# Gate modulation sums moved into the attention steps, and a negated causal mask applied together with the row extreme, in a two-layer trunk on one Trainium2 core

## The chip, the cores and the metric

The kernel runs on one core of a Trainium2 chip. That core has a matrix engine (PE, whose weight loads the profile lists as PEld), a vector engine (DVE), a scalar engine (ACT), a general engine (POOL) and a sync engine (SP), which here issues most of the DMAs; sixteen DMA engines carry the transfers. The metric is the device time of one execution in microseconds (us), lower being better, as the median of three runs.

## The reference

Two layers over a sequence of 512 tokens of width 2048, batch 1, all in f32. Layer 1 is a multi-scale retention, layer 2 a latent attention; each is one residual sub-layer, and shift, scale and gate of each layer come from a conditioning vector c of 2048 numbers.

```
mod  = silu(c) @ ada_w[i] + ada_b[i]          # shift, scale, gate of layer i
h    = rmsnorm(x, g) * (1 + scale) + shift
x    = x + gate * branch(h)                   # branch: retention, or attention
```

The attention (16 heads, 128 "nope" and 64 rotary dimensions a head, values of 128) is

```
q  = rmsnorm(cq) @ w_uq ; k_nope, v = split(rmsnorm(ckv) @ w_ukv)
s  = (q @ k.T) * 192 ** -0.5
s  = where(key_pos <= query_pos, s, -1e30)
o  = softmax(s) @ v
out = (silu(g) * o) @ w_out
```

The gate of layer 2 is a vector of 2048 numbers, each a sum of 2048 products of silu(c) with a column of ada_w.

## The kernel before

The program is written step by step, and the issue order on every engine is the order in which the steps are written; `queued(...)` writes one operation down, and `behind(engine)` puts an operation where that engine's queue stands. f32 products are made from a high and a low part, so nearly every matmul comes three times (`mm3`, lines L158 to L160) and a tile that feeds PE is first split by ACT (high part, L1937) and DVE (low part, L1938: the source less the high part).

Layer 2's attention works on pairs of heads. `attention_step(pr)` treats heads 2pr and 2pr+1 and, between their parts, makes the projections of the next pair, nx = pr + 1. `attention_step(-1)`, in which there are no heads yet, makes only the projections of pair 0; then follow steps 0 to 6. The last pair's heads are interleaved with the output projection, which ends the kernel.

The projections of a pair are seven PSUM tiles, in this order: uq_2 (the rotary part of both heads' q), uq_0, uq_1 (the other q), uk_0, uk_1 (k) and uv_0, uv_1 (v). They take turns on four PSUM buffers ("acc"), so uk_1 takes the buffer of uq_2, uv_0 that of uq_0 and so on. The rotation of uq_2 is three pieces: `rope_own` (DVE, L1949: qr_t = uq_2 * cos), `rope_swap` (ACT, L1944: four copies of 32 rows from uq_2 into qr_sw) and `rope_turn` (DVE, L1953 and L1954: qr_sw * sin, then the sum). The buffer of uq_2 is free when both qr_t and the four copies have read it. In the built program the first of the four copies waits for qr_t.

A head's scores s fill four PSUM tiles a_0 to a_3 (query blocks of 128 rows, 128 to 512 key columns; "aux" buffers). For each, DVE adds the 128x128 causal mask to the block on the diagonal (L2084) and takes the negated row maximum (L2086), and ACT makes exp(s + that) with the row sums (L2087). After the four tiles come the reciprocals (L2091), the normalisation, the transposes on PE, their split (pt, L1937 and L1938) and the products with v.

Layer 2's gate is made from ada_w's transpose: 16 blocks of 128 outputs by two halves of 1024 inputs are 32 tiles of 128x1024 (512 KB, `mod_gate`, two buffers), each loaded by SP (L2153) and multiplied by the half of silu(c) that stands in `c_gate` (broadcast to 128 rows, loaded by L2147) and summed along the row by one DVE operation (`gate_sum`, L2157). The first 16 sums ("part 0") stand in the attention steps -1 to 6, two in each, ahead of the two splits of the values (`part_values`) at the step's end; their loads are issued at the step's start. The other 16 ("part 1") stand in the output projection (`o2_hooks`).

Of the kernel before, what the change touches and what calls it, by code (L numbers as in the profile page):

```python
# [49 lines left out]
def hybrid_trunk_kernel(  # L50
# [25 lines left out]
    nc = tc.nc  # L76
    PE, ACT, DVE, POOL = nc.tensor, nc.scalar, nc.vector, nc.gpsimd
# [17 lines left out]
    def big(name, dt=F32R):  # L95
        return base.tile([P, 2, T], dt, tag="big", bufs=16, name=name)
# [19 lines left out]
    ident = base.tile([P, P], F32, name="ident")  # L116
    make_identity(nc, ident)
    mask = base.tile([P, P], F32, name="mask")
    make_causal_mask(nc, mask, mask_val=-1e30)
    ones = base.tile([P, P], F32, name="ones")  # L120
    DVE.memset(ones, 1.0)
    few = base.tile([P, 2 * NT], F32, name="few")
# [92 lines left out]
    qn_c, kvn_c = vcol[:, 128:132], vcol[:, 132:136]  # L215
# [244 lines left out]
    A_, V_, T_, S_ = (getattr(mybir.EngineType, e) for e in ("Activation", "DVE", "PE", "SP"))  # L460

    @contextmanager
    def behind(*engines):

        with ExitStack() as stack:
            for e in engines:
                ins = next((i for i in reversed(nc.cur_bb.bb.instructions) if i.engine == e), None)
                if ins is not None:
                    stack.enter_context(tc.issue_after(ins))
            yield  # L470

    def queued(fn, *args):
        with behind(A_, V_, T_, S_):
            return fn(*args)
# [256 lines left out]
    for u in range(1, NU):  # L731

        here, there = ("v", "qk") if u % 2 == 0 else ("qk", "v")
# [989 lines left out]
    def l2_tile(tag, bufs, name, shape=(P, T), dt=F32):  # L1723
        return pools["l2"].tile(list(shape), dt, tag=tag, bufs=bufs, name=name)
# [121 lines left out]

    def latent_norm(n):
        if n == "q":
            DVE.tensor_scalar(out=qn_s, in0=qn_c, scalar1=192.0**-0.5, scalar2=None, op0=ALU.mult)
        ss = small(f"ss_{n}", NT)  # L1850
        for t in range(NT):
            ACT.activation(tmp(f"{n}_sq{t}"), latent[n][t], AF.Square, accum_out=ss[:, t : t + 1])
        latent[n, "ss"] = ss
# [207 lines left out]
    def attend(h):  # L2061

        pr, s = h // 2, h % 2
        own = heads2[pr]
        ps, p_, nb, pt, side = [], [], [], [], {}

        def scores(i):
            n = (i + 1) * P
            ps.append(aux(f"a_{h}_{i}"))
            qn, kn, qr = own["uq", s, "T"], own["uk", s, "T"], own["qr"]  # L2070
            mm3(ps[i][:, :n], act_block(qn, i), (kn[:, 0, :n], kn[:, 1, :n]), True, False)
            for a in range(2):
                PE.matmul(ps[i][:, :n], qr[:, s, i * P : n], krope[0][:, a, :n], start=False, stop=a == 1)

        def exps(i):
            n = (i + 1) * P
            if i == 0:
                side["sm"] = small(f"sm_{h}", NT)
                if s == 0:
                    p_.extend(l2_tile("pp", 5, f"p_{h}_{j}") for j in range(NT))  # L2080
                else:
                    both = l2_pair(f"p_{h}_").bitcast(F32)
                    p_.extend(both[:, j * T : (j + 1) * T] for j in range(NT))
            DVE.tensor_add(ps[i][:, i * P : n], ps[i][:, i * P : n], mask)  # L2084
            nb.append(small(f"nb_{h}_{i}"))
            DVE.tensor_reduce(out=nb[i], in_=ps[i][:, :n], axis=AX.X, op=ALU.max, negate=True)  # L2086
            ACT.activation(p_[i][:, :n], ps[i][:, :n], AF.Exp, bias=nb[i], accum_out=side["sm"][:, i : i + 1])  # L2087

        def reciprocals():
            side["rs"] = small(f"rs_{h}", NT)  # L2090
            DVE.reciprocal(side["rs"], side["sm"])  # L2091

        def normalise():
            for i in range(NT):
                v, r = p_[i][:, : (i + 1) * P], side["rs"][:, i : i + 1]
                if s == 0:
                    ACT.activation(v, v, AF.Identity, scale=r)
                else:
                    DVE.tensor_scalar(out=v, in0=v, scalar1=r, scalar2=None, op0=ALU.mult)

        place = [(0, 0), (1, 0), (2, 0), (1, 384)]

        def transposes():
# [25 lines left out]

        def result():  # L2130
            o2 = l2_tile("o2", 2, f"o2_{h}")
            DVE.tensor_mul(o2, side["o"], side["sg"])
            POOL.dma_start(o2_d[h * P : (h + 1) * P, :], o2)

        return scores, exps, lambda: (queued(reciprocals), queued(normalise)), transposes, split_pt, load_gate, values, result

    gate_c_half = {}
    gate_sums = [base.tile([P, 2, 8], F32, tag="mod_c", bufs=2, name=f"gate_sums{i}") for i in range(2)]  # L2140

    def gate_load(part, n):

        j, b = n // 8, n % 8
        if b == 0:
            half = gate_c_half[j] = big(f"c_gate{part}{j}", F32)
            nc.sync.dma_start(  # L2147
                half.rearrange("p a n -> p (a n)"),
                c_d[0:1, j * 1024 : (j + 1) * 1024].rearrange("o n -> (o n)").partition_broadcast(P),
            )  # L2150
        aw = l2_tile("bw", 2, f"mod_gate_{part}{b}{j}", (P, 2, T))
        r0 = 2 * D + (8 * part + b) * P
        nc.sync.dma_start(aw, ada_t[1, r0 : r0 + P, j * 1024 : (j + 1) * 1024].rearrange("p (a n) -> p a n", a=2))  # L2153
        return aw, part, j, b, gate_c_half[j]

    def gate_sum(aw, part, j, b, c_half):
        DVE.scalar_tensor_tensor(  # L2157
            out=aw, in0=aw, scalar=1.0, in1=c_half, op0=ALU.mult, op1=ALU.mult,
            accum_out=gate_sums[part][:, j, b : b + 1],
        )  # L2160
        if (j, b) == (1, 7):
            use_modulation(1, 2, part, gate_sums[part])

    def attention_step(pr):

        nx = pr + 1
        here = [attend(2 * pr + s) for s in range(2)] if pr >= 0 else ()
        both = heads2[nx] = {}
        units_ahead()
        with behind(S_):  # L2170
            sums = [gate_load(0, 2 * nx + i) for i in range(2)]
        if here:
            (sc0, ex0, no0, tr0, sp0, lg0, va0, re0), (sc1, ex1, no1, tr1, sp1, lg1, va1, re1) = here
            queued(lg0)
# [7 lines left out]
        low()  # L2182
        if here:
            no0()
        queued(uq_products, nx, 2)
        if here:
            for i in range(NT):
                queued(sc1, i)
            for i in range(NT):
                queued(ex1, i)  # L2190
        t1 = queued(rope_own, both["uq", 2], f"qr_{nx}")
        low = next_unit("ukv") if here else lambda: None
        if here:
            no1()
        low()
        for b in range(2):
            queued(uq_products, nx, b)
        sw = queued(rope_swap, both["uq", 2], f"qr_{nx}")
# [26 lines left out]
            queued(uv_products, nx, j, (1,))  # L2225
        for j in range(2):
            queued(uv_products, nx, j, (0, 2, 3))
            queued(gate_sum, *sums[j])
            queued(queued(part_values, nx, j))
        if here:  # L2230
            queued(va1)
# [3 lines left out]
        krope.append(big("kr"))  # L2235
        split(kr["f"], krope[0][:, 0, :], krope[0][:, 1, :])

    first = Step(multiply=lambda: (queued(krope_parts), attention_step(-1)))
    first.units = [unit("ukv", 0, 0)]
    steps[-1].units += [unit("uq", 0, u) for u in range(2)]  # L2240
    steps.append(first)
# [121 lines left out]
    o2_in, o2_res = {}, {}  # L2363
    N_ENDS = 5

    gate_pending, gate_n = [], [0, 0]

    def o2_hooks(i):
        l2_hooks.get(i, lambda: None)()
        with behind(V_):  # L2370
            while gate_pending:
                gate_sum(*gate_pending.pop())
        with behind(S_):
            for _ in range(min(1, 16 - gate_n[0]) if 4 < i and i > gate_n[1] else 0):
                gate_pending.insert(0, gate_load(1, gate_n[0]))
                gate_n[0] += 1
        gate_n[1] = i

    def o2_parts(r, u):
        if u not in o2_in:  # L2380
# [235 lines left out]
```

## Time and the profile before

| what | value |
|---|---|
| three runs | 2119.31, 2120.16, 2120.32 us; median 2120.16 us |
| profiled execution, span of the core | 2118.4 us |
| PE busy | 2104.0 us (99%) |
| DVE busy | 1676.0 us (79%) |
| ACT busy | 1055.5 us (50%) |
| attention_step(-1) on PE | about 1677 to 1696.5 us |
| steps 0 to 6 | about 1697.5 to 1918.6 us |
| output projection with the last pair | about 1918.6 to 2106 us |

The page gives no time of its own for the profiled execution beside its span; the span is 1.8 us under the median of the runs, which is time around the span. In the answers of the trace, a timeline row is: start, duration, engine, line, operation, tile written from tiles read, shapes, count, and, in brackets, for how long the engine sat idle before it and what ended that. A DMA's row on SP is its issue and not its transfer; how long the transfer took from its issue until it had landed is a row of another view. Matmuls overlap in the records, so PE's steps are read from their starts.

### The profile page before, as it was taken

Reading aid. Unit: us, or ns where it says so; the run is one execution under the profiler, and the core shown is the slowest. Engines: PE = TensorE matmul, PEld = TensorE weight load, DVE = VectorE, ACT = ScalarE, POOL = GpSimd, SP = SyncE. Lnnn points to the kernel's source line nnn. Section 1 sums busy time; section 2 is a strip of 40 time slices with the busy share of each in tenths; the row PEclk is TensorE's granted clock in tenths of the full one; section 3 lists DMA queues with packets and bytes.
Section 4 is the critical chain, followed back from the end, with each engine's and each line's share of the span. In section 5 each row is a group of like instructions: output and inputs, shape, how many; then the busy total and the mean of one; then the engine's idle time right before and its main releaser. Section 6 shows DMA issues by size and latency. Waiting matters only on the chain.

```text
span 2118.4 us, 30062 instructions
## 1 busy us (share of the span) xinstructions
PE 2104.0 (99%) x11124; PEld 1812.6 (86%) x11124; DVE 1676.0 (79%) x2506; ACT 1055.5 (50%) x1622; POOL 103.6 (5%) x176
## 2 busy tenths in 40 slices
PE   8999999999999999999999999999999999999998
PEld 6888898989889888888888888898889989888888
DVE  7899888888888789666777778768978788886665
ACT  6765444444454444434344444345446575664443
POOL 1001010000000000000000000010001000000000
PEclk9999999999999999999999999999999999999999
DMA  9975786868787778856657556753566644346643
GB/s 381 406 280 195 248 276 222 283 211 272 239 263 250 242 229 283 265 172 196 222 173 241 201 198 230 258 191 108 164 189 209 190 129 149 118 137 219 222 142 138
DMA packets 230101, 462.95 MB, mean 219 GB/s; under 512 B 20881, under 2 KB 84401, under 8 KB 226369
## 3 DMA queue, kind: packets, MB, share of 16 engines
q1 hardware_dynamic: 217312, 421.07, 60.3%
q0 software_dynamic: 11920, 38.91, 4.7%
q8 instruction: 87, 1.43, 0.3%
q10 hardware_dynamic: 722, 1.06, 0.2%
q14 instruction: 60, 0.49, 0.1%
HBM read 417.96 MB, written 43.00 MB: 218 GB/s over the span
## 4 chain that ended last, share of the span: by engine, by line
PE 96%; DMA 1%; DVE 1%; ACT 0%; issue 0%; SPq 0%; DVEq 0%
PE o L1486 16%; PE o L2450 4%; PE x L884 2%; PE x L883 2%; PE x L885 2%; PE y L885 2%; PE y L884 2%; PE s L885 2%; PE s L884 2%; PE s L883 2%; PE y L883 2%; PE uv L2046 2%; PE qk L158 2%; PE s_qk L984 2%; PE x_qk L984 2%; PE qk L160 2%
## 5 line engine op out<-in xcount | busy, mean ns | idle before, releaser
L1486 PE MATMUL o<-o_h,o_p 128*128 128x512 f32 (+1 forms) x1088 | 323.0, 378 | 0.0
L1486 PEld LDWEIGHTS o<-o_h,o_p 128*128 128x128 f32 x1088 | 200.2, 188 | 37.1
L1486 PE MATMUL o<-o_l,o_p 128*128 128x512 f32 (+1 forms) x544 | 204.8, 376 | 0.0
L136 DVE TENSOR_TENSOR o_p<-o_r,o_p 128x1024 fp32r<-128x1024 f32 x64 | 78.1, 1222 | 54.3 <-ACT o_p L135 54.1
L1486 PEld LDWEIGHTS o<-o_l,o_p 128*128 128x128 f32 x544 | 102.3, 188 | 18.3
L2450 PE MATMUL o<-o_h,o_w 128*128 128x512 f32 (+1 forms) x336 | 82.7, 337 | 0.0
L1170 DVE SCALAR_TENSOR_TENSOR mod<-mod,c_odd 128x1024 f32<-128x1024 f32 x56 | 67.2, 1219 | 15.3 <-DMA mod<-in_ada_t_dram 15.3
L135 ACT CAST o_p<-o_r 128x1024 fp32r<-128x1024 f32 x64 | 66.7, 1054 | 22.4 <-PE o L1486 13.3
L158 PE MATMUL qk<-hT,qk_p 128*128 128x512 f32 x192 | 75.0, 391 | 0.0
L160 PE MATMUL qk<-hT,qk_p 128*128 128x512 f32 x192 | 74.9, 390 | 0.0
L389 DVE SCALAR_TENSOR_TENSOR aw<-aw,c_all 128x2048 f32<-128x2048 f32 (+1 forms) x37 | 73.2, 1997 | 2.1 <-DMA aw<-in_ada_t_dram 2.1
L159 PE MATMUL qk<-hT,qk_p 128*128 128x512 f32 x192 | 74.7, 389 | 0.0
L2450 PEld LDWEIGHTS o<-o_h,o_w 128*128 128x128 f32 x336 | 57.7, 188 | 6.9
L2450 PE MATMUL o<-o_l,o_w 128*128 128x512 f32 (+1 forms) x168 | 56.5, 337 | 0.0
L136 DVE TENSOR_TENSOR o_l<-o_in,o_h 128x1024 fp32r<-128x1024 f32 x24 | 29.3, 1222 | 34.2 <-ACT o_h L135 34.2
L1332 ACT ACTIVATE yn<-y,nmr,gn_r 128x512 f32<-128x512 f32 x32 | 22.3, 778 | 67.7 <-DVE nmr L1326 67.7
L135 ACT CAST o_h<-o_in 128x1024 fp32r<-128x1024 f32 x24 | 25.3, 1052 | 61.6 <-PE o L159 40.5
L158 PE MATMUL o<-o_h,o_w 128*128 128x512 f32 x128 | 50.1, 391 | 0.0
L160 PE MATMUL o<-o_h,o_w 128*128 128x512 f32 x128 | 49.8, 389 | 0.0
L159 PE MATMUL o<-o_l,o_w 128*128 128x512 f32 x128 | 49.8, 389 | 0.0
L1170 DVE SCALAR_TENSOR_TENSOR mod<-mod,c_bm 128x1024 f32<-128x1024 f32 x40 | 48.7, 1219 | 0.0
L448 PE MATMUL g<-hT,g_p 128*128 128x512 f32 x192 | 46.1, 389 | 0.0
(1532 smaller groups left out, 6238.3 us busy)
## 6 DMA issues: line engine op xcount, KB each, us to landing
mod<-in_ada_t_dram SPq DMA_DIRECT2D x96, 512.0 KB, 5.7
o_r<-in_ret_w_out_dram SPq DMA_DIRECT2D x64, 512.0 KB, 5.5
aw<-in_ada_t_dram SPq DMA_DIRECT2D x28, 1024.0 KB, 9.5
mod_gate<-in_ada_t_dram SPq DMA_DIRECT2D x32, 512.0 KB, 4.4
o_w_raw<-in_mla_w_out_dram SPq DMA_DIRECT2D x32, 512.0 KB, 4.4
qk_r<-in_ret_w_in_dram SPq DMA_DIRECT2D x48, 256.0 KB, 3.5
qk_r<-qk_d SPq DMA_DIRECT2D x32, 256.0 KB, 6.1
v_r<-v_d SPq DMA_DIRECT2D x32, 256.0 KB, 5.7
```

The costliest lines, as they stand in the source:

```text
L135: ACT.copy(hi, src)
L136: DVE.tensor_sub(lo, src, hi.bitcast(F32))
L158: PE.matmul(o, lhs[0], rhs[0], start=first and not seeded, stop=False, skip_group_check=seeded)
L159: PE.matmul(o, lhs[0], rhs[1], start=False, stop=False, skip_group_check=seeded)
L160: return PE.matmul(o, lhs[1], rhs[0], start=False, stop=last, skip_group_check=seeded)
L883: PE.matmul(banks[b], a[0], w[0], start=first, stop=False, skip_group_check=True)
L884: PE.matmul(banks[b], a[0], w[1], start=False, stop=False, skip_group_check=True)
L885: PE.matmul(banks[b], a[1], w[0], start=False, stop=True, skip_group_check=True)
L984: PE.matmul(o, w[wp][:, i, b * P : (b + 1) * P], a[ap], start=first and i + b + k == 0, stop=k == 2, skip_group_check=True,)
L1170: DVE.scalar_tensor_tensor(out=aw, in0=aw, scalar=1.0, in1=silu_c[j], op0=ALU.mult, op1=ALU.mult, accum_out=row_sums[piece][:, j, b : b + 1],)
L1486: PE.matmul(o, w[i][:, ki, c0 + b * P : c0 + (b + 1) * P], a[j], start=first and i + j == 0, stop=last and i == 1, skip_group_check=True,)
L2450: PE.matmul(banks2[b][:, cols], w[0][i][:, 0, b * P : (b + 1) * P], o2_moving(w, u, cols)[j], start=u + i + j == 0, stop=u == KD - 1 and i ...
```

## The change

Three things are changed in layer 2.

First, q is scaled by the negated factor, so that the score tiles hold negated scores; the mask holds +1e30, and one DVE operation (`tensor_tensor_reduce`) adds a mask to all columns of the tile, in place, and takes the row minimum, in place of L2084 and L2086; the exponential takes scale -1. The mask for all widths is one tile `masks` of 384 columns of zeros and 128 columns of the causal mask, of which each query block reads the last n columns. It stands in one of the five buffers "pp", which hold p of a pair's first head, and is filled in step -1 by a POOL memset and an ACT copy. In the order of the program the new operation is a row `ISA` with the tile, and a second with the row extreme (`nb`) alone.

Second, all 32 gate sums are in steps -1 to 6, four in each: the first ahead of the products of uq_2, the second in the middle of the second head's four mask operations, and the third and fourth where the two stood before. In step -1, where there are no heads, the first two follow each other.

Third, the loads follow a list: up to two tiles are on their way at a time, issued at the step's start, in its middle and behind each of the third and fourth sums. The 32 tiles go through one half of c for both parts and then through the other, so c_gate is loaded twice and not four times.

```diff
@@ def latent_norm(n)
-            DVE.tensor_scalar(out=qn_s, in0=qn_c, scalar1=192.0**-0.5, scalar2=None, op0=ALU.mult)
+            DVE.tensor_scalar(out=qn_s, in0=qn_c, scalar1=-(192.0**-0.5), scalar2=None, op0=ALU.mult)
@@ def attend(h), exps(i)
-            DVE.tensor_add(ps[i][:, i * P : n], ps[i][:, i * P : n], mask)
             nb.append(small(f"nb_{h}_{i}"))
-            DVE.tensor_reduce(out=nb[i], in_=ps[i][:, :n], axis=AX.X, op=ALU.max, negate=True)
-            ACT.activation(p_[i][:, :n], ps[i][:, :n], AF.Exp, bias=nb[i], accum_out=side["sm"][:, i : i + 1])
+            DVE.tensor_tensor_reduce(
+                out=ps[i][:, :n], in0=ps[i][:, :n], in1=masks[0][:, T - n :], scale=1.0, scalar=3e38, op0=ALU.add,
+                op1=ALU.min, accum_out=nb[i],
+            )
+            ACT.activation(
+                p_[i][:, :n], ps[i][:, :n], AF.Exp, bias=nb[i], scale=-1.0, accum_out=side["sm"][:, i : i + 1]
+            )
@@ gate loads and sums
-    def gate_load(part, n):
-        j, b = n // 8, n % 8
-        if b == 0:
-            half = gate_c_half[j] = big(f"c_gate{part}{j}", F32)
+    gate_n, gate_pending = [0], []
+    def gate_load():
+        n = gate_n[0]
+        j, part, b = n // 16, n // 8 % 2, n % 8
+        if n % 16 == 0:
+            half = gate_c_half[j] = big(f"c_gate{j}", F32)
...
+    def gate_loads():
+        with behind(S_):
+            while gate_n[0] < 32 and len(gate_pending) < 2 and not (gate_n[0] % 16 == 0 and gate_pending):
+                gate_load()
+
+    def gate_sum():
+        aw, part, j, b, c_half = gate_pending.pop(0)
         DVE.scalar_tensor_tensor(
...
+    def make_masks():
+        masks.append(l2_tile("pp", 5, "masks"))
+        POOL.memset(masks[0][:, : T - P], 0.0)
+        ACT.copy(masks[0][:, T - P :], mask)
@@ def attention_step(pr)
-        with behind(S_):
-            sums = [gate_load(0, 2 * nx + i) for i in range(2)]
+        gate_loads()
...
         if here:
             no0()
+        queued(gate_sum)
         queued(uq_products, nx, 2)
         if here:
             for i in range(NT):
                 queued(sc1, i)
-            for i in range(NT):
+            for i in range(2):
+                queued(ex1, i)
+        queued(gate_sum)
+        if here:
+            for i in range(2, NT):
                 queued(ex1, i)
         t1 = queued(rope_own, both["uq", 2], f"qr_{nx}")
         low = next_unit("ukv") if here else lambda: None
         if here:
             no1()
         low()
+        gate_loads()
...
         for j in range(2):
             queued(uv_products, nx, j, (0, 2, 3))
-            queued(gate_sum, *sums[j])
+            queued(gate_sum)
+            gate_loads()
             queued(queued(part_values, nx, j))
@@ def o2_hooks(i)
-        with behind(V_):
-            while gate_pending:
-                gate_sum(*gate_pending.pop())
-        with behind(S_):
-            for _ in range(min(1, 16 - gate_n[0]) if 4 < i and i > gate_n[1] else 0):
-                gate_pending.insert(0, gate_load(1, gate_n[0]))
-                gate_n[0] += 1
-        gate_n[1] = i
```

The first place is DVE's queue in step -1, from the split of the rotary key (kr) to the split of uq_0. Before:

```order
L136 TENSOR_TENSOR kr<-kr_f,kr 128x512
L1938 TENSOR_TENSOR ukv_1_p<-ukv_1_r,ukv_1_p 128x2x256 x2
L1949 TENSOR_TENSOR qr_t_15096<-uq_2_15083,cos_12566 128x512
L1953 TENSOR_TENSOR qr_sw<-qr_sw,sin_12568 128x512
L1954 TENSOR_TENSOR qr_t_15096<-qr_t_15096,qr_sw 128x512
L1938 TENSOR_TENSOR uqT_0_15129<-uq_0_15098,uqT_0_15129 128x512
```

The same place with the change:

```order
L136 TENSOR_TENSOR kr<-kr_f,kr 128x512
L1938 TENSOR_TENSOR ukv_1_p<-ukv_1_r,ukv_1_p 128x2x256 x2
L2170 SCALAR_TENSOR_TENSOR mod_gate_15075,gate_sums_1426<-mod_gate_15075,c_gate_15073 128x1024
L2170 SCALAR_TENSOR_TENSOR mod_gate_15077,gate_sums_1426<-mod_gate_15077,c_gate_15073 128x1024
L1949 TENSOR_TENSOR qr_t_15101<-uq_2_15087,cos_12566 128x512
L1953 TENSOR_TENSOR qr_sw<-qr_sw,sin_12568 128x512
L1954 TENSOR_TENSOR qr_t_15101<-qr_t_15101,qr_sw 128x512
L1938 TENSOR_TENSOR uqT_0_15138<-uq_0_15107,uqT_0_15138 128x512
```

Two gate sums now stand between the split of ukv_1 and qr_t, and so ahead of everything that follows on DVE in this step. SP's queue from this step's start is, with the change (c_gate, here `L2153`, stands third in both kernels, behind the step's first two mod_gate tiles; the two mod_gate tiles behind ukv_0 are the third and fourth of the step):

```order
L2159 DMA mod_gate_15075<-in_ada_t_dram 128x1024
L2159 DMA mod_gate_15077<-in_ada_t_dram 128x1024
L2153 DMA c_gate_15073<-c_d 128x1024
L1974 DMA ukv_0_r<-in_mla_w_ukv_dram 128x2x512
L2159 DMA mod_gate_15103<-in_ada_t_dram 128x1024
L2159 DMA mod_gate_15105<-in_ada_t_dram 128x1024
L1974 DMA ukv_1_r<-in_mla_w_ukv_dram 128x2x512
L1974 DMA uq_0_r<-in_mla_w_uq_dram 128x2x384
```

The second pair of mod_gate tiles stood behind uq_0 before, and now stands between two loads of projection weights.

The second place is DVE's queue in a pair's step (step 1), from the reciprocals of the first head to the rotation of the next pair. Before:

```order
L2091 RECIPROCAL rs_15670<-sm_15645 128x4
L2084 TENSOR_TENSOR a_0_15689<-a_0_15689,mask 128x128
L2086 TENSOR_REDUCE nb_0_15716<-a_0_15689 128x1
L2084 TENSOR_TENSOR a_1_15695<-a_1_15695,mask 128x128
L2086 TENSOR_REDUCE nb_1_15720<-a_1_15695 128x1
L2084 TENSOR_TENSOR a_2_15701<-a_2_15701,mask 128x128
L2086 TENSOR_REDUCE nb_2_15724<-a_2_15701 128x1
L2084 TENSOR_TENSOR a_3_15707<-a_3_15707,mask 128x128
L2086 TENSOR_REDUCE nb_3_15728<-a_3_15707 128x1
L1949 TENSOR_TENSOR qr_t_15731<-uq_2_15676,cos_12566 128x512
```

With the change, where `ISA` is the new mask operation and `L2170` the gate sum:

```order
L2095 RECIPROCAL rs_15673<-sm_15652 128x4
L2170 SCALAR_TENSOR_TENSOR mod_gate_15576,gate_sums_1427<-mod_gate_15576,c_gate_15073 128x1024
L2085 ISA a_0_15693,nb_0_15719<-a_0_15693,masks 128x128
L2085 ISA nb_0_15719 128x1
L2085 ISA a_1_15699,nb_1_15722<-a_1_15699,masks 128x256
L2085 ISA nb_1_15722 128x1
L2170 SCALAR_TENSOR_TENSOR mod_gate_15600,gate_sums_1427<-mod_gate_15600,c_gate_15073 128x1024
L2085 ISA a_2_15705,nb_2_15726<-a_2_15705,masks 128x384
L2085 ISA nb_2_15726 128x1
L2085 ISA a_3_15711,nb_3_15729<-a_3_15711,masks 128x512
L2085 ISA nb_3_15729 128x1
L1949 TENSOR_TENSOR qr_t_15732<-uq_2_15680,cos_12566 128x512
```

Two operations a score tile have become one with its read-out, and two sums have come in ahead of qr_t.

More of the change, by code (lines that the diff above doesn't have):

```diff
@@ L118, in hybrid_trunk_kernel @@
     mask = base.tile([P, P], F32, name="mask")
-    make_causal_mask(nc, mask, mask_val=-1e30)
+    make_causal_mask(nc, mask, mask_val=1e30)
     ones = base.tile([P, P], F32, name="ones")
@@ L2153, in gate_load @@
         nc.sync.dma_start(aw, ada_t[1, r0 : r0 + P, j * 1024 : (j + 1) * 1024].rearrange("p (a n) -> p a n", a=2))
-        return aw, part, j, b, gate_c_half[j]
-    def gate_sum(aw, part, j, b, c_half):
+        gate_n[0] += 1
+        gate_pending.append((aw, part, j, b, gate_c_half[j]))
+    def gate_loads():
[4 more added lines that the diff above has]
+        aw, part, j, b, c_half = gate_pending.pop(0)
         DVE.scalar_tensor_tensor(
@@ L2162, in gate_sum @@
             use_modulation(1, 2, part, gate_sums[part])
+    masks = []
+    def make_masks():
+        masks.append(l2_tile("pp", 5, "masks"))
+        POOL.memset(masks[0][:, : T - P], 0.0)
+        ACT.copy(masks[0][:, T - P :], mask)
     def attention_step(pr):
@@ L2236, in krope_parts @@
         split(kr["f"], krope[0][:, 0, :], krope[0][:, 1, :])
-    first = Step(multiply=lambda: (queued(krope_parts), attention_step(-1)))
+    first = Step(multiply=lambda: (queued(krope_parts), queued(make_masks), attention_step(-1)))
     first.units = [unit("ukv", 0, 0)]
@@ L2364, in hybrid_trunk_kernel @@
     N_ENDS = 5
-    gate_pending, gate_n = [], [0, 0]
     def o2_hooks(i):
         l2_hooks.get(i, lambda: None)()
-        with behind(V_):
-            while gate_pending:
-                gate_sum(*gate_pending.pop())
-        with behind(S_):
-            for _ in range(min(1, 16 - gate_n[0]) if 4 < i and i > gate_n[1] else 0):
-                gate_pending.insert(0, gate_load(1, gate_n[0]))
-                gate_n[0] += 1
-        gate_n[1] = i
     def o2_parts(r, u):
```

## The prediction

> **What bounds the kernel now.** I read the page's busy shares first, then two stretches of the trace (a pair's step; the output projection), then all of PE's waits.
>
> ```profile
> PE 2104.0 (99%) x11124; PEld 1812.6 (86%) x11124; DVE 1676.0 (79%) x2506; ACT 1055.5 (50%) x1622; POOL 103.6 (5%) x176
> ...
> 1760.69:1792.27 31.58, 31.58 (x195) 28.43 (x194) 26.07 (x54) 20.02 (x46) 1.08 (x2) 1.00 0.45 142
> 1918.56:2060.00 141.44, 141.44 (x651) 118.26 (x650) 94.52 (x126) 63.57 (x87) 1.63 (x3) 1.00 0.59 196
> ...
> PE c_ps L474 <- DMA c_all<-in_c_dram: 3.2, 1, 3.2
> PE xT_ps L474 <- DVE x_diag L571: 2.2, 3, 1.2
> PE v L448 <- DVE hT L423: 0.9, 1, 0.9
> PE y L158 <- DVE o_l L1366: 0.3, 1, 0.3
> PE x_sums L2483 <- ACT x_sq L2422: 0.2, 1, 0.2
> ```
>
> The second and third rows are stretches: length, then busy time of PE, PEld, DVE, ACT and POOL, granted clock, DMA share. A pair's step is 31.58 us long and PE is busy through all of it at clock 1.00; DVE is busy for 26.07. The output projection is PE from end to end too. The last five rows are all of PE's waits in the whole run, 6.8 us together, and only the 0.2 at the very end lies behind the touched code. So PE sets the end everywhere that the change reaches: DVE work taken away is worth nothing there, and only a new PE wait can move the time.
>
> **The change part by part.** First place, step -1. DVE's, ACT's, SP's and PE's rows of it before:
>
> ```profile
> 1680.62 1.29 DVE L1938 TENSOR_TENSOR ukv_p<-ukv_r,ukv_p 128x512 fp32r<-128x512 f32 x2
> 1681.82 0.68 DVE L1949 TENSOR_TENSOR qr_t<-uq,cos 128x512 f32<-128x512 f32 x1
> ...
> 1686.26 1.28 DVE L1938 TENSOR_TENSOR uqT<-uq,uqT 128x512 fp32r<-128x512 f32 x2
> ...
> 1682.54 2.35 ACT L1944 COPY qr_sw<-uq 32x512 f32<-32x512 f32 x4 [1.52 <-DVE qr_t L1949]
> ...
> 1687.99 0.39 PE L160 MATMUL uk<-kvT,ukv_p 128*128 128x512 f32 x1
> 1688.22 0.39 PE L158 MATMUL uk<-kvT,ukv_p 128*128 128x512 f32 x1
> ...
> 1676.05 2.12 SPq L2153 DMA_DIRECT2D mod_gate<-in_ada_t_dram  x2
> 1678.21 0.49 SPq L2147 DMA_DIRECT2D c_gate<-c_d  x1
> 1681.93 0.38 SPq L1974 DMA_DIRECT2D ukv_r<-in_mla_w_ukv_dram  x1
> ```
>
> PE's row at 1688.22 is the first of uk_1, which takes uq_2's buffer; the one ahead is the last of uk_0. The buffer is free when ACT's four copies into qr_sw are done, and ACT's row says what these waited for: 1.52 us, for qr_t. Before, qr_t started at 1681.82 and the copies ended at 1682.54 + 2.35 = 1684.89, 3.3 us ahead of uk_1. The change puts two gate sums ahead of qr_t, and the first needs mod_gate and c_gate. When have those landed? Transfers around c_gate's issue, each with its time from issue to landing, and last the landings known for c_gate in the whole run (three of its four):
>
> ```profile
> mod_gate<-in_ada_t_dram SPq DMA_DIRECT2D x1, 512.0 KB, 7.1
> ...
> mod_gate<-in_ada_t_dram SPq DMA_DIRECT2D x1, 512.0 KB, 7.8
> ...
> ukv_r<-in_mla_w_ukv_dram SPq DMA_DIRECT2D x1, 512.0 KB, 7.4
> ...
> DMA to landing us min/median/max: 5.6/5.6/8.0
> ```
>
> The two mod_gate tiles, issued at 1676.05 and just before 1678.2 (I take 1677.7), landed at 1683.15 and about 1685.5; ukv_r, the transfer behind c_gate, issued at 1681.93, landed at 1689.33. They landed in order of issue, so c_gate lies between 1685.5 and 1689.3. The two mod_gates are 2.35 apart; one such step behind the second is 1687.85, my value. The sums' own time comes from two that follow each other at once:
>
> ```profile
> 33.24 1.22 DVE L389 SCALAR_TENSOR_TENSOR aw<-aw,c_all 128x1024 f32<-128x1024 f32 x1
> 34.38 0.08 DVE L389 DVE_READ_ACCUMULATOR aw<-aw,c_all 128x1 f32 x1
> 34.38 1.22 DVE L389 SCALAR_TENSOR_TENSOR aw<-aw,c_all 128x1024 f32<-128x1024 f32 x1
> ```
>
> 1.14 us from start to start, so 2.3 for two. Then: sums from 1687.85, qr_t at 1690.2 instead of 1681.82, the first copy 0.72 later as before (1682.54 - 1681.82) at 1690.9, all four done at 1693.25, uk_1 at 1693.3 instead of 1688.22. **PE stands for 5.1 us**; with the landing at its bounds, 2.75 to 6.55. Late next: DVE's splits of uq_0 and uq_1, which free the buffers of uv_0 and uv_1. They come 8.4 us later, the first done at about 1686.26 + 0.64 + 8.4 = 1695.3, and uv_0 starts behind uk_1's 12 matmuls of 0.227 us, at 1696.0: 0.7 to spare. Behind that PE has no idle time that could give 5.1 us back, so it reaches the end.
>
> Second place, steps 0 to 6. Groups over those seven steps and the page's row of a wide product:
>
> ```profile
> L2086 DVE TENSOR_REDUCE nb<-a 128x1 f32<-128x128 f32 (+3 forms) x56 | 27.5, 491 | 1.9
> ...
> L2157 DVE SCALAR_TENSOR_TENSOR mod_gate<-mod_gate,c_gate 128x1024 f32<-128x1024 f32 x14 | 17.0, 1214 | 0.0
> L2084 DVE TENSOR_TENSOR a<-a,mask 128x128 f32<-128x128 f32 x56 | 16.7, 297 | 10.5 <-PE a L2073 9.0
> ...
> L136 DVE TENSOR_TENSOR o_p<-o_r,o_p 128x1024 fp32r<-128x1024 f32 x64 | 78.1, 1222 | 54.3 <-ACT o_p L135 54.1
> ```
>
> Removed a step: 8 x 0.297 + 8 x 0.491 = 6.30 us. Added: two sums, 2.28, and eight of the new operation, which no row shows. From below it is a reduction of the same columns and a read-out, 0.491 + 0.08: 4.57 for eight. From above, twice that pass, as if the sum and the minimum took the columns one after the other: 0.98 + 0.08, 8.5 for eight. I take the lower end, since a one-pass sum with a row sum (1.214 for 1024 columns) costs no more than a plain product (1.222). DVE goes from 26.07 to 26.6 us of 31.58, or to 30.55 at the upper end: hidden by PE either way, with 5.0 or 1.0 to spare.
>
> [...]
>
> Within a step, what is late is qr_t, and with it all that DVE does up to pt, the transposed probabilities:
>
> ```profile
> 1765.16 0.17 DVE L2091 RECIPROCAL rs<-sm 128x4 f32<-128x4 f32 x1
> ...
> 1776.72 1.61 DVE L1938 TENSOR_TENSOR pt<-pT,pt 128x512 fp32r<-128x512 f32 x3
> ...
> 1780.76 0.39 PE L158 MATMUL o<-pt,v 128*128 128x512 f32 x1
> ...
> 1755.11 3.56 SPq L2153 DMA_DIRECT2D mod_gate<-in_ada_t_dram  x2
> ...
> DMA to landing us min/median/max: 4.1/4.6/5.8
> ...
> 1773.51 8.31 SPq L1974 DMA_DIRECT2D ukv_r<-in_mla_w_ukv_dram  x2
> ```
>
> pt is done at 1778.33, 2.4 us ahead of the first product that reads it. Up to there the mask operations of both heads save 6.30 - 4.57 = 1.7 and the two sums cost 2.3: 0.6 late, inside 2.4. The first two sums (behind the reciprocal, 1765.3) read tiles issued at 1755.11 and 3.3 us later; landings of mod_gate in these steps take 4.1 to 5.8 (the last row but one), so they are there by 1764.2. The next two tiles are issued in the step's middle, where the buffers come free by 1768, behind ukv_r's first issue at 1773.51, and land by 1780; their sums stand at 1785. SP queues one load of weights behind them, two issues or 0.7 us later.
>
> The negated scale, the exponential's scale and the mask's fill in step -1 (384 columns on POOL, 128 on ACT, idle for 1.52 us just there) cost nothing measurable, nor does the tile that `masks` takes from "pp": four are left, as many as a pair's first head fills. Two broadcasts less, and 16 sums (16 x 1.14 = 18.2 us of DVE) and 8 MB less in the output projection, are worth nothing, because PE waits for nothing there.
>
> Sum: the profiled span 2118.4 + 5.1 = 2123.5. The runs' median stands 1.8 above the span, so **2125.3**.
>
> **Rivals.** *The clock falls in the gap.* PE's end shows the granted clock with PE idle:
>
> ```profile
> 2107.44 3.69 PE L2545 MATMUL y_ps<-ident,x 128*128 128x128 f32 x32
> ...
> 2113.00:2114.00 1.00, 0.00 (x0) 0.00 (x0) 0.00 (x0) 0.00 (x0) 0.00 (x0) 1.00 1.05 385
> 2114.00:2116.00 2.00, 0.00 (x0) 0.00 (x0) 0.00 (x0) 0.00 (x0) 0.00 (x0) 0.73 1.05 312
> ...
> 16.79 4.07 PE L474 MATMUL xT_ps<-x_diag,x 128*128 128x128 f32 x16 [0.48 <-DVE x_diag L571]
> ...
> 22.36 2.04 PE L474 MATMUL xT_ps<-x_diag,x 128*128 128x128 f32 x16
> ```
>
> PE's last work ends at 2111.1; the clock is 1.00 up to 2114 and 0.73 on average over the next two, which a fall to 0.50 at 2114.9 makes: 3.8 us after. A 5.1 us gap is longer. How long full speed then takes to return, the start shows: 16 transposes in 4.07 us at 16.79, the same 16 in 2.04 at 22.36, so up to 5.6 us of work at half speed, half of which is lost: +2.8, to **2128.1**. Against it: one fall is all that I have, and a smaller gap would not reach it.
>
> [...]
>
> *Not slower.* If qr_t weren't held, the time would stay: for that c_gate must have landed by 1688.22 - 0.05 - 2.35 - 0.72 - 2.3 = 1682.8, 4.6 us after its issue. Its known landings (5.6, 5.6, 8.0) are all longer and give 1683.8 and 1686.2, or stalls of 1.0 and 3.4, so half the way is open: **2120.2 to 2123**, at worst for my forecast no change.
>
> *The steps overrun.* If the new operation takes three times the reduction (8 x 1.55 = 12.4), DVE needs 34.5 us in a step, 2.9 more than PE, seven times: 20 us, **2145**. It decides from (31.58 - 26.6) / 8 = 0.62 us more per operation. Against it, the two passes with two sources quoted above take 1.2 ns a column, with a sum of the row or without (1214 and 1222 for 1024).
>
> *Faster.* It would need PE to stop waiting somewhere, and the five waits lie elsewhere.
>
> **How the numbers follow.** 0.50 for the stall of 5.1 alone, whose own range is 2122.9 to 2126.7 by c_gate's bounds; 0.30 for the stall with the clock's fall; 0.10 for an early landing; 0.07 for an overrun; 0.03 for faster. The range reaches from 2122.3, under the smallest stall, to 2129.5, a stall of 6.5 and most of the clock's loss. No change means within 0.2%, 4.2 us, about what a measurement can tell here; a stall under 4.2, which the lower bounds of c_gate give, counts there too. So faster 0.04, same 0.16, slower 0.80.
>
> **What would show it.** In the changed profile: a PE wait of about 5 us at the first matmul of uk_1, near 1688, put down to ACT's qr_sw or to DVE's qr_t; the first gate sum behind a DMA wait that ends near 1687.9, and qr_t 2.3 us behind it; PE busy through the steps, 31.6 us each; DVE near 26.6 in each; the new operation near 0.5 us on average; the granted clock below 1.00 right behind the gap only if the rival holds. I am wrong if PE doesn't wait near 1688, if a step grows beyond 31.7, or if the output projection shrinks.

## The result and the profile after

The changed kernel takes 2126.68 us (median of five runs, 2125.90 to 2129.48) against 2120.16 before (five runs, 2119.31 to 2120.32): a ratio of 1.0035, 95% interval 1.0024 to 1.0046. It is slower by 6.5 us. The profiled execution took 2127.37, with a span of 2125.6, 7.2 over the span before.

The three longest of PE's waits, and then DVE's, ACT's and PE's rows of step -1 in the changed kernel (timeline rows, as before: start, duration, engine, line, operation, tiles; idle time and its releaser in brackets):

```profile
PE uk L158 <- ACT qr_sw L1944: 5.0, 1, 5.0
PE xT_ps L474 <- DVE x_diag L571: 3.1, 3, 2.0
PE c_ps L474 <- DMA c_all<-in_c_dram: 2.5, 1, 2.5
...
1687.18 1.23 DVE L2170 SCALAR_TENSOR_TENSOR mod_gate<-mod_gate,c_gate 128x1024 f32<-128x1024 f32 x1 [5.92 <-DMA c_gate<-c_d]
1688.33 0.08 DVE L2170 DVE_READ_ACCUMULATOR mod_gate<-mod_gate,c_gate 128x1 f32 x1
1688.33 1.22 DVE L2170 SCALAR_TENSOR_TENSOR mod_gate<-mod_gate,c_gate 128x1024 f32<-128x1024 f32 x1
1689.48 0.08 DVE L2170 DVE_READ_ACCUMULATOR mod_gate<-mod_gate,c_gate 128x1 f32 x1
1689.48 0.68 DVE L1949 TENSOR_TENSOR qr_t<-uq,cos 128x512 f32<-128x512 f32 x1
...
1690.19 2.34 ACT L1944 COPY qr_sw<-uq 32x512 f32<-32x512 f32 x4 [9.74 <-DVE qr_t L1949]
...
1687.23 0.39 PE L160 MATMUL uk<-kvT,ukv_p 128*128 128x512 f32 x1
1692.59 0.80 PE L158 MATMUL uk<-kvT,ukv_p 128*128 128x512 f32 x1 [4.97 <-ACT qr_sw L1944]
1693.18 0.63 PE L159 MATMUL uk<-kvT,ukv_p 128*128 128x512 f32 x1
1693.61 0.63 PE L160 MATMUL uk<-kvT,ukv_p 128*128 128x512 f32 x1
```

The chain is read upward: PE's first matmul of uk_1 waited 4.97 us for ACT's copies, these for qr_t, qr_t stood behind two gate sums on DVE, and the first of these waited for c_gate. The wait at the top of the list is new; the others are those of the kernel's start, as before. One more thing stands in PE's rows: the matmuls after the gap are 0.43 us apart (1693.18 to 1693.61) where those ahead of it were 0.23. The stretches of this place (length, busy time of PE, PEld, DVE, ACT, POOL, then the granted clock) say why:

```profile
1691.00:1692.00 1.00, 0.00 (x0) 0.00 (x0) 0.00 (x0) 0.98 (x3) 0.00 (x0) 0.91 0.72 266
1692.00:1693.00 1.00, 0.41 (x1) 0.42 (x2) 0.43 (x1) 0.98 (x2) 0.00 (x0) 0.50 0.64 234
1697.00:1698.00 1.00, 1.00 (x4) 0.79 (x3) 1.00 (x3) 0.00 (x0) 0.00 (x0) 0.50 0.00 0
1698.00:1699.00 1.00, 1.00 (x8) 1.00 (x7) 0.54 (x2) 0.89 (x3) 0.00 (x0) 0.68 0.00 0
1699.00:1700.00 1.00, 1.00 (x10) 1.00 (x10) 1.00 (x3) 0.52 (x2) 0.00 (x0) 1.00 0.52 139
```

The clock fell to half at about 1691.8, while PE stood, and came back at 1698.6, so PE worked from 1692.59 to 1698.64 at half speed and lost 3.0 us. The gap cost 5.13 (1692.59 - 1687.23 - 0.23). Together 8.1; PE had come to this point 0.76 us earlier than in the profile before (1687.23 and 1687.99), which leaves 7.4 for a span that grew by 7.2. Most of the 0.76 arises in layer 1, which the change does not touch: at 1203.76 PE waits for DVE's o_l in the profile before, and not in this one.

The rest of the program did not move. The pair's step that was shown before (7.27 us later here), and the groups of the new operation over the seven steps:

```profile
1767.96:1799.54 31.58, 31.58 (x195) 28.43 (x194) 26.14 (x58) 20.02 (x46) 1.08 (x2) 1.00 0.53 176
...
L2170 DVE SCALAR_TENSOR_TENSOR mod_gate<-mod_gate,c_gate 128x1024 f32<-128x1024 f32 x28 | 33.9, 1211 | 0.0
L2085 DVE CUSTOM_DVE_ANT_0 a<-a,masks 128x128 f32<-128x128 f32 (+3 forms) x56 | 27.5, 499 | 9.4 <-PE a L2073 8.4
L2085 DVE DVE_READ_ACCUMULATOR2_ANT nb<- 128x1 f32 x56 | 7.9, 141 | 0.0
```

The step is 31.58 us long as before, with PE busy throughout; DVE is busy for 26.14 in place of 26.07. The new operation takes 499 ns on average, where the row extreme alone took 491, and its read-out 141.

### The profile page after: what moved, and what is told of

It reads as the page before. It is cut to its first block, busy times and chain, and to the rows that moved or that the text cites. A ratio compares the mean times of both kernels' runs of the same rounds, so it can differ in the third digit from the quotient of the medians.

```text
span 2125.6 us, 30065 instructions
## 1 busy us (share of the span) xinstructions
PE 2104.4 (99%) x11124; PEld 1812.3 (85%) x11124; DVE 1659.5 (78%) x2506; ACT 1055.5 (50%) x1623; POOL 103.7 (5%) x177
## 4 chain that ended last, share of the span: by engine, by line
PE 95%; DMA 3%; DVE 0%; ACT 0%; SPq 0%; issue 0%; DVEq 0%; ACTq 0%
PE o L1486 16%; PE o L2466 4%; PE x L884 2%; PE x L883 2%; PE y L884 2%; PE s L884 2%; PE y L883 2%; PE s L883 2%; PE x L885 2%; PE s L885 2%; PE y L885 2%; PE uv L2046 2%; PE qk L158 2%; PE s_qk L984 2%; PE x_qk L984 2%; PE qk L160 2%
## 5 line engine op out<-in xcount | busy, mean ns | idle before, releaser
L136 DVE TENSOR_TENSOR o_w<-o_w_raw,o_w 128x1024 fp32r<-128x1024 f32 x32 | 38.9, 1219 | 13.4 <-ACT o_w L135 13.3
```

Of the source, the lines that this page charges most:

```text
L136: DVE.tensor_sub(lo, src, hi.bitcast(F32))
```

## The experiments

Each is compared with runs of the kernel before on its own chip (their median in brackets), so that the differences count and not the times.

**The two sums behind the rotation.** In step -1 alone, the first two gate sums go behind the rotation of q.

```diff
-        queued(gate_sum)
+        if here:
+            queued(gate_sum)
         queued(uq_products, nx, 2)
...
-        queued(gate_sum)
         if here:
+            queued(gate_sum)
             for i in range(2, NT):
                 queued(ex1, i)
...
         queued(rope_lows, t1, both["qr"])
+        if not here:
+            queued(gate_sum)
+            queued(gate_sum)
+            gate_loads()
```

> The changed kernel with its first two gate sums of step -1 put behind the rotation of q (behind the lows of qr); all else as changed, 32 sums and the new mask operation included. Theory S (the two sums ahead of qr_t hold PE at uk_1, and the gap lets the clock fall): no PE wait near 1688, and the time is that of before, 2120.2, within 0.8. Rival N (the 6.5 us come from the new operation, the added sums in the pairs' steps or the moved loads): the time stays near 2126.7.

Measured: 2119.45 (before 2119.45), ratio 1.0000, interval 0.9991 to 1.0009. DVE's rows of step -1 in this kernel:

```profile
1680.80 0.68 DVE L1949 TENSOR_TENSOR qr_t<-uq,cos 128x512 f32<-128x512 f32 x1
...
1686.55 1.40 DVE L1965 TENSOR_TENSOR qr<-qr_t,qr 64x512 fp32r<-64x512 f32 x2
1687.98 1.23 DVE L2170 SCALAR_TENSOR_TENSOR mod_gate<-mod_gate,c_gate 128x1024 f32<-128x1024 f32 x1
1689.13 0.08 DVE L2170 DVE_READ_ACCUMULATOR mod_gate<-mod_gate,c_gate 128x1 f32 x1
1689.13 1.22 DVE L2170 SCALAR_TENSOR_TENSOR mod_gate<-mod_gate,c_gate 128x1024 f32<-128x1024 f32 x1
```

qr_t is back at its old place, right behind the split, the sums come 7 us behind it, and c_gate has landed when DVE gets to the first (no idle time ahead of it). The whole loss is in the place of two of 32 sums. All else that the change does, the mask operation, the 30 other sums, the moved loads and the lightened output projection, is worth nothing within 0.9 in 1000. This version is as fast as the kernel before, not faster: PE has no wait left there to remove.

**The mask part alone, and the gate part alone.** The first is the kernel before with the change's edits to the q scale, the mask, `exps` and `masks`; the second is the changed kernel with these undone:

```diff
-            DVE.tensor_tensor_reduce(
-                out=ps[i][:, :n], in0=ps[i][:, :n], in1=masks[0][:, T - n :], scale=1.0, scalar=3e38, op0=ALU.add,
-                op1=ALU.min, accum_out=nb[i],
-            )
...
+            DVE.tensor_add(ps[i][:, i * P : n], ps[i][:, i * P : n], mask)
+            DVE.tensor_reduce(out=nb[i], in_=ps[i][:, :n], axis=AX.X, op=ALU.max, negate=True)
...
```

The lines left out set back the signs of q, of the mask and of the exponential, and the fill of `masks`.

> The kernel before with the mask part of the change alone (negated scale, one operation for mask and row extreme, masks tile). Theory S: 2120.2 within 0.8, with DVE about 1.3 us less busy in a pair's step than before (26.07). Rival N (the new operation or its fill costs time): up to 2126.7.

> The changed kernel with the old mask addition and row maximum: the gate part of the change alone. Theory S: as the changed kernel, 2126.7 within 1.5, with the PE wait of 5 us at uk_1. Rival N by the new operation: nearer to 2120.2.

Measured: mask alone 2119.30 (2119.45), ratio 0.9999, interval 0.9990 to 1.0008. Gates alone 2126.77 (2119.45), ratio 1.0033, interval 1.0021 to 1.0045, with PE's wait in place:

```profile
PE uk L158 <- ACT qr_sw L1944: 4.4, 1, 4.4
```

So the loss belongs to the gate part, and the mask part makes none of it that these intervals could show. The mask part alone leaves DVE busy for 24.11 us of a pair's step in place of 26.07, and the time does not move.

**Matmuls in the gap.** Twenty matmuls that nobody reads, between uk_0 and uk_1 of step -1, keep PE at work while it would wait.

```diff
+    def filler(pr):
+        ps = aux("filler")
+        a, b = w_block(unit_parts["uq", pr, 0], 0, 0), act_row(latent["q", "T"][0])
+        for n in range(20):
+            PE.matmul(ps, a[0], b[0], start=True, stop=True)
...
         for b in range(2):
+            if b and not here:
+                queued(filler, nx)
             queued(uk_products, nx, b)
```

> The changed kernel with 20 matmuls more on PE, whose result nobody reads, between uk_0 and uk_1 of step -1 (20 x 0.227 = 4.5 us, so they end ahead of the wait's end). Theory S with the clock's fall as a cost of its own: the wait for qr_sw shrinks to about 0.6, uk_1 starts as late as in the changed kernel, but at full clock, so the time falls by the 1 to 3 us that the half clock cost: 2124 to 2125.3, that is before + 5.1 or a little less. Rival S0 (the stall alone, no price of the clock): 2126.7 as changed, or longer if the matmuls don't fit in the gap.

Measured: 2123.98 (2119.45), ratio 1.0022, interval 1.0013 to 1.0031. That is 4.5 over before, and 2.8 under the gate part alone on the same chip, with more work on PE. PE's and ACT's rows:

```profile
1686.93 4.69 PE L2188 MATMUL filler<-qT,uq_h 128*128 128x512 f32 x20
...
1689.19 2.35 ACT L1944 COPY qr_sw<-uq 32x512 f32<-32x512 f32 x4 [9.26 <-DVE qr_t L1949]
```

The copies end at 1691.54 and uk_1 starts at 1691.59, 4.66 us after the place where it would have started (1686.93): the stall is all there. What is gone is the half clock; the clock's record has no fall in this run ahead of the kernel's end (1.00 in every stretch from 1687 to 1701). The loss of the gate part, 7.3 us, is thus two things, about 4.6 us of standing and 2.8 of half clock.

**What the sums wait for.** Two ways to take c_gate out of the wait. The first loads c for the two sums a step earlier into a buffer of its own; the second makes the two sums multiply their tile with itself, so that they need no c:

```diff
+    def load_early_c():
+        early_c.append(l2_tile("pt", 4, "early_c", (P, 2, T), F32R).bitcast(F32))
+        nc.sync.dma_start(early_c[0]...)
+    g23[-2].beside["form"].append(lambda: load_early_c())
...
-        if n % 16 == 0:
+        if n in (2, 16):
             half = gate_c_half[j] = big(f"c_gate{j}", F32)
...
-        gate_pending.append((aw, part, j, b, gate_c_half[j]))
+        gate_pending.append((aw, part, j, b, gate_c_half[j] if n > 1 else early_c[0]))
```

```diff
-            out=aw, in0=aw, scalar=1.0, in1=c_half, op0=ALU.mult, op1=ALU.mult,
+            out=aw, in0=aw, scalar=1.0, in1=aw if part == 0 and j == 0 and b < 2 else c_half, op0=ALU.mult, op1=ALU.mult,
```

> The changed kernel with c for the two sums of step -1 loaded ahead into a buffer of its own (a step earlier), and c_gate's own load behind ukv_0, ahead of the third sum; the sums keep their place ahead of qr_t. Theory S: the second mod_gate lands near 1685.5, two us ahead of c_gate, so qr_t starts near 1686.7, uk_1 near 1689.8, and PE waits 1.5 us with the clock left at 1.00: 2121.7, between 2120.5 and 2123. If the two sums' place alone made the price, whatever they wait for: 2126.7.

> The changed kernel with the first two sums multiplying their tile with itself instead of with c (so two columns of the gate's sums are left out and the gate comes out other than the reference); c_gate is loaded as before, and the DMA queues are those of the changed kernel. Theory S: the sums wait for their own tiles alone, landing near 1683 and 1685.5, so qr_t starts near 1686.7 and PE waits about 1.5 us at uk_1 (0.5 to 2.5, by the tiles' landing); with under 2 us of idle the clock stays up in every run: before + 1.5, 2121, and the spread of the runs is that of before, about 1.5. If c_gate's landing isn't what the first sum waits for: 2126.7 as changed.

The first missed its forecast: 2127.28 (2119.20), ratio 1.0034, interval 1.0021 to 1.0047. SP's and DVE's rows tell why:

```profile
1671.85 0.34 SPq L2151 DMA_DIRECT2D early_c<-c_d  x1
...
1673.30 6.60 SPq L1976 DMA_DIRECT2D uq_r<-in_mla_w_uq_dram  x2
1679.95 0.93 SPq L2168 DMA_DIRECT2D mod_gate<-in_ada_t_dram  x2
...
1685.38 1.22 DVE L2179 SCALAR_TENSOR_TENSOR mod_gate<-mod_gate,early_c 128x1024 f32<-128x1024 f32 x1 [1.46 <-DMA mod_gate<-in_ada_t_dram]
...
1687.48 1.23 DVE L2179 SCALAR_TENSOR_TENSOR mod_gate<-mod_gate,early_c 128x1024 f32<-128x1024 f32 x1 [0.87 <-DMA mod_gate<-in_ada_t_dram]
```

Ahead of the first row, the early load's issue, SP's queue stood for 6.7 us, a wait put down to PE, and the loads behind it were late in turn: the mod_gate tiles were issued from 1679.95 on and not at 1675.2 to 1677.3 as in the changed kernel, and now these came last. The edit swapped one late tile for another and cannot tell what c_gate's wait is worth. The second leaves the queues as they are: 2120.88 (2119.64), ratio 1.0008, interval 0.9999 to 1.0017, PE's wait 1.3 us and no fall of the clock in the profiled run:

```profile
PE uk L158 <- ACT qr_sw L1944: 1.3, 1, 1.3
...
1681.92 1.23 DVE L2170 SCALAR_TENSOR_TENSOR mod_gate<-mod_gate 128x1024 f32<-128x1024 f32 x1 [0.38 <-DMA mod_gate<-in_ada_t_dram]
...
1684.88 1.23 DVE L2170 SCALAR_TENSOR_TENSOR mod_gate<-mod_gate 128x1024 f32<-128x1024 f32 x1 [1.73 <-DMA mod_gate<-in_ada_t_dram]
1686.03 0.09 DVE L2170 DVE_READ_ACCUMULATOR mod_gate<-mod_gate 128x1 f32 x1
1686.03 0.69 DVE L1949 TENSOR_TENSOR qr_t<-uq,cos 128x512 f32<-128x512 f32 x1
```

So the wait for c_gate, with the half clock that follows from it, is most of the loss: without it qr_t starts 3.5 us sooner, and 1.2 of the change's 6.5 us are left. Two of its eleven runs (2122.88 and 2124.20) lie well above the rest; they have no trace, and whether a tile landed late or the clock fell there is open.

**The gap's length.** One sum ahead of qr_t in place of two, the other behind the rotation; and three, the second tile once more:

```diff
-        queued(gate_sum)
         if here:
+            queued(gate_sum)
...
         queued(rope_lows, t1, both["qr"])
+        if not here:
+            queued(gate_sum)
+            gate_loads()
```

```diff
-        queued(gate_sum)
+        last = queued(gate_sum)
+        if not here:
+            queued(extra_sum, *last)
...
```

> The changed kernel with only one of the two sums of step -1 ahead of qr_t, and the second behind the rotation. Theory S: the wait shrinks by one sum, 1.14 us, to 3.9, and PE starts again before the 3.8 to 4.2 us at which the clock was seen to fall: 2124 without a fall, so 2.6 under the changed kernel. If the clock falls after any gap of this size: 2125.5 to 2127. If the wait for c_gate were no part of it, half of the 6.5 would go: 2123.4.

> The changed kernel with a third sum on DVE ahead of qr_t (the second tile once more, its result unused). Theory S: the wait grows by 1.14 us to about 6.2 and the clock falls in every run: 2127.8 to 2129. If the gap's length past the fall costs nothing more: 2126.7.

Measured: one sum 2126.20 (2119.20), ratio 1.0032, interval 1.0019 to 1.0044, with PE's wait at 3.25 us; three sums 2128.05 (2119.20), ratio 1.0043, interval 1.0029 to 1.0056, with a wait of 5.8. The wait went with the number of sums, as expected, but with one sum the median did not fall to 2124 (one of its five runs did, 2124.08, and has no trace): in the profiled run the clock fell in this gap too.

```profile
1687.76 0.39 PE L160 MATMUL uk<-kvT,ukv_p 128*128 128x512 f32 x1
1691.41 0.79 PE L158 MATMUL uk<-kvT,ukv_p 128*128 128x512 f32 x1 [3.25 <-ACT qr_sw L1944]
...
1690.00:1691.00 1.00, 0.00 (x0) 0.00 (x0) 0.00 (x0) 0.98 (x3) 0.00 (x0) 0.82 0.87 324
1691.00:1692.00 1.00, 0.59 (x2) 0.50 (x3) 0.61 (x1) 0.98 (x3) 0.00 (x0) 0.50 0.21 82
...
1697.00:1698.00 1.00, 1.00 (x9) 1.00 (x9) 1.00 (x3) 1.00 (x3) 0.00 (x0) 0.77 0.37 33
```

It fell at 1690.63, 2.5 us after PE's last matmul (1687.76 + 0.39), where the end of the program had shown 3.8. So it is no fixed delay. Here are all profiled gaps of this place, with the fall and return by the clock's record in the trace. "PE lost" is the pitch over a full-speed matmul at the gap, plus half the time that PE worked at half clock; "measured" is the profiled execution's time over the median of the kernel before in the same comparison (with c loaded early the profiled execution is the fastest of five, whose median is 8.1 over):

| kernel | PE's wait | clock fell, after PE's last matmul | at half clock | PE lost: gap + clock | measured |
|---|---|---|---|---|---|
| no c | 1.3 | no | - | 1.4 + 0 | 1.6 |
| one sum | 3.3 | 2.5 | 6.83 | 3.4 + 3.0 | 7.0 |
| c loaded early | 4.0 | 3.8 | 3.41 | 4.2 + 1.6 | 6.0 |
| gates alone | 4.4 | 2.9 | 6.83 | 4.6 + 2.7 | 7.5 |
| the change | 5.0 | 4.2 | 6.83 | 5.1 + 3.0 | 7.2 |
| three sums | 5.8 | 5.0 | 6.83 | 6.0 + 3.0 | 9.5 |

The two terms add up to the measured loss within a microsecond. In these five falls the delay varies from 2.5 to 5.0 us, but the time at half clock is 3.41 us or twice that.

**The clock by itself.** A kernel that leaves out the whole computation and writes zeros: bursts of 60 to 70 matmuls, with gaps between them that a chain of DVE operations makes.

```python
for rep in range(6):
    for g in GAPS:                      # columns of the DVE operation in the gap
        ...                             # rhs waits for a DVE chain that starts from "end"
        for m in range(60 + 2 * rep):
            PE.matmul(ps, w, rhs, start=True, stop=True)
        DVE.tensor_copy(end, ps[:, :1])
```

> A kernel that leaves out the whole computation and writes zeros: 66 bursts of 60 to 70 matmuls of 512 columns, each held until a DVE chain of one of 11 lengths behind the burst ahead is done, so PE idles for about 1 to 7 us, each length six times. [...]

This first form made no gaps: nothing tied the DVE chain to the burst ahead, DVE ran ahead of PE, and PE never waited after its first burst (its only wait in the run is one of 6.1 us). In the second the chain starts from that burst's result:

> A kernel that leaves out the whole computation and writes zeros: 90 bursts of 60 to 70 matmuls of 512 columns, each held until a chain of DVE operations that starts from the burst ahead's result is done, with 15 lengths of the chain, so PE idles for about 1.5 to 6.5 us, each length six times. From the five gaps in the attention kernels (3.3 to 5.8 us, all with a fall, half clock for 3.41 or 6.83 us): a grid of windows of 3.41 us that runs freely, a fall at a window's end where PE was busy for less than about a quarter of it, a return at the end of the next window in which it was busy for nearly all. Then gaps under 2.5 us never lead to a fall, gaps of 3 to 3.4 in some of the cases, those over 5.9 always; and every piece at half clock lasts 3.41 or 6.83 us. A timer from the last matmul instead: one sharp length that decides, and pieces of any duration.

The gaps came out at 0.9 to 5.2 us of idle time, shorter than meant, so none tests the forecast for those over 5.9. Here are all 89, with the idle time as the profile shows it, and whether the clock fell:

| idle, us | 0.9 to 1.7 | 2.0 | 2.3 | 2.5 | 2.8 | 3.1 | 3.3 | 3.6 | 3.9 to 5.2 |
|---|---|---|---|---|---|---|---|---|---|
| gaps | 17 | 6 | 6 | 6 | 6 | 6 | 6 | 6 | 30 |
| with a fall | 0 | 4 | 3 | 4 | 3 | 4 | 6 | 5 | 30 |

Of the 59 pieces at half clock, 40 last 3.41 us and 19 last 6.83, none anything else. Three bursts of 60 matmuls in a row, the first two behind gaps with a fall and the third behind a longer one without:

```profile
55.26 15.47 PE L109 MATMUL ps<-rhs,w 128*128 128x512 f32 x60 [1.99 <-DVE rhs L103]
72.99 15.36 PE L109 MATMUL ps<-rhs,w 128*128 128x512 f32 x60 [2.26 <-DVE rhs L103]
90.87 13.86 PE L109 MATMUL ps<-rhs,w 128*128 128x512 f32 x60 [2.52 <-DVE rhs L103]
```

The gap of 1.99 us with a fall cost the burst behind it 1.6 us more (15.47 against 13.86). A timer from the last matmul is out: there is no sharp length that decides (most lengths from 2.0 to 3.6 us have gaps with a fall and gaps without), and the pieces have two lengths only. Falls and returns lie on a grid of 3.41 us: all 59 falls and the returns behind them keep the same place on it within 4 ns over the whole run, whatever PE did.

What parts the gaps is how much of one window of that grid PE stood idle. Laid over the 89 gaps, the grid parts them without an exception: the 59 gaps that put at least 1.92 us of idle time into one window have a fall, the 30 that put at most 1.90 into any have none. So gaps of 2.0 that lay within a window had a fall, and one of 3.6, which the grid cut into 1.90 and 1.69, had none; over twice 1.91, 3.8 us, no cut leaves both parts under 1.91, and the 30 gaps from 3.9 on all have a fall. Of the 30 gaps between 2.0 and 3.1 us, each shorter than the 3.41 of a window, 18 had one. The attention kernels agree: a window with 1.25 us of idle time (no c) and one with 1.6 (the first that the gap with three sums touches) brought no fall, and one with 2.48 did (one sum, 1687.22 to 1690.63, with PE busy to about 1688.1). The length at half clock goes with the grid too: one window where PE stood idle for at most 0.62 us of the window behind the fall (40 pieces), two where it stood idle for longer (19); in the attention kernels 0.20 gave one window, 0.77 to 1.47 gave two.

The forecast had the grid and the pieces right and the threshold too high: gaps under 2.5 us were never to lead to a fall, and 7 of the 12 at 2.0 and 2.3 did; PE was to be busy for less than about a quarter of the window, and by the 1.91 us of idle time less than 0.44 of it was enough.

## Why the prediction was right

The measured 2126.68 lies in the range of 2122.3 to 2129.5 and on the side that was given 0.80, but the single number, 2125.3, stands for a case that isn't the one that occurred. Step by step:

- **PE sets the end, so relief elsewhere is worth nothing.** Right. The output projection lost 16 sums and 8 MB of loads, the pairs' steps gained two sums each, and with the two early sums put back the time is that of before (ratio 1.0000).
- **Step -1: the sums wait for c_gate, qr_t for the sums, the copies for qr_t, uk_1 for the copies.** Right in each link, and in size: 5.1 forecast, 5.1 measured in the profiled run of the change, 4.6 in that of the gate part alone. c_gate landed 9.8 us after its issue (1677.36 to 1687.18) where 9.6 was forecast (1678.21 to 1687.85). This landing varies: in the four other profiles in which the first sum waits for c_gate it took 9.1 to 9.3 us.
- **Nothing further is late.** Right: no other wait of PE behind 1700 is new. uv_0, with 0.7 us to spare by the forecast, had about 3.3 (the split done near 1694.5, uv_0 at 1697.87), since uk_1's 12 matmuls took 5.1 us at half clock and not 2.7.
- **The steps.** Right: DVE is busy for 26.14 us against 26.6 forecast, of 31.58. The new operation is at the lower bound (499 ns against 491 of the reduction). Its read-out, 141 ns, is longer than the 80 taken, but in the step shown the next operation, where it waits for nothing, starts with the read-out (both at 1770.90, at 1774.50 and at 1776.80) or before its end (1776.18 against 1776.13 + 0.14).
- **The clock.** Here the choice was wrong. The rival "the clock falls in the gap" had 0.30 and 2.8 us; it occurred in each of the five profiled gaps from 3.3 to 5.8 us, and it cost 2.8 between the kernels with and without matmuls in the gap. The price came out, although it was read from another stretch (5.6 us at half speed at the kernel's start, where here it is one window of 3.41 us or two). The chance was too low: the prediction had one fall to go by, at the program's end, 3.8 us after PE's last work, and held that a smaller gap would not reach it. The gap of 3.3 us did, and from 3.9 us on every gap of the bursts has a fall (30 of 30), so the stall of 5.1 alone was not a likely case at all.
- **The number.** That 2125.3 lies only 1.4 us off is in part luck. It leaves out 2.8 us for the clock; the two terms together gave 2128.1, 1.4 over the measured median. The stall was nearer 4.6 than 5.1 in one of the two profiles that show it, and the half clock lasted one window of 3.41 us in one of the five profiled gaps and two in four, by where the gap happened to lie on the grid.

## What to carry to other kernels

Work that is added to an engine's queue because that engine has time to spare still delays whatever is queued behind it (here qr_t, from 1681.82 to 1689.48), and in a step without the usual waits it may itself wait for a load that was issued for later use (here 5.92 us for c_gate): look for the first instruction behind it that frees a PSUM buffer. Where PE never stops, price a new stop as its length plus the clock: in the five profiled gaps with a fall, of 3.3 to 5.8 us, the clock took 1.6 to 3.0 us of work; in the bursts it fell in 29 of 42 gaps from 2.0 to 3.6 us, by how the gap lay on the grid of 3.41 us, and in all 30 from 3.9 on. A load put ahead of others in a queue holds them up if it must itself wait before it can be issued: with c loaded early the queue stood for 6.7 us ahead of that load, and the mod_gate tiles were issued from 1679.95 on in place of 1675.22.

## What was not expected of the hardware

In the bursts the clock fell after gaps as short as 2.0 us (4 of 6), in every gap from 3.9 us on (30 of 30), and in none up to 1.7 (17 gaps); it came back after 3.41 or 6.83 us and nothing else (40 and 19 of 59 pieces). Whether at least about 1.9 us of idle time fell into one window of 3.41 us parts all 89 gaps. In the kernel, with PE busy for 99% of the span, a wait of 3.3 us had the same price in clock as one of 5.0, 3.0 us on top of the gap in both profiled runs.
